# Making the high and low parts of the feed-forward weights with casting and accumulating DMAs

## The chip, the core and the metric

The kernel runs on one core of a Trainium2 chip. The core has TensorE (PE in the profile) for matrix multiplies, VectorE (DVE) and ScalarE (ACT) for elementwise work, GpSimd (POOL) for small odd work, and SyncE (SP), which here only issues DMAs. Each engine works through its own queue in order, and they meet through semaphores. Sixteen DMA engines move data between memory and the on-chip SBUF. POOL can issue DMAs too. The metric is the time of one execution on the device, in microseconds.

## The reference

One transformer-like block over 512 tokens of width 1024, in float32:

```python
h = rms_norm(x, norm1_g[l])
proj = h @ w_in[l]
...
merged = (jax.nn.sigmoid(g_ssd) * (y_ssd @ w_ssd_proj[l])
          + jax.nn.sigmoid(g_attn) * (y_attn @ w_attn_proj[l]))
x = x + merged @ w_out[l]
h2 = rms_norm(x, norm2_g[l])
u = causal_dwconv(h2 @ w_up[l], ffn_conv_w[l], ffn_conv_b[l])
u_gate, u_val = jnp.split(u, 2, axis=-1)
x = x + (jax.nn.silu(u_gate) * u_val) @ w_down[l]
```

The first half has a state-space branch and a windowed attention branch. The change touches only the weights of the last part, the feed-forward: w_up (1024 by 5632) and w_down (2816 by 1024).

## The kernel before

All large products are made with three matrix multiplies in the type float32r, a float32 with a shortened mantissa: each operand is split into a high part, its value rounded to float32r, and a low part, the rest. The product is high·high + high·low + low·high, summed in one PSUM bank. Activations are split once and stay in SBUF (h2h and h2l after the second norm, acth and actl after the gate). Weights are streamed.

The stream is a list of *pieces* of 512 KB (128 partitions by 1024 values), in the order in which TensorE uses them. Pieces 0 to 127 belong to the earlier stages, 128 to 171 to w_up (128 columns each, read from memory in rows of 128 values), 172 to 193 to w_down (256 rows by 512 columns each, in rows of 512 values). `load_piece` (L85) loads a piece through SP's queue into a tile called raw. `make_piece` (L91) casts it on ACT to the high part whi (L100) and subtracts on DVE to the low part wlo (L101). Each of the three kinds of tile has three buffers, so a piece's parts take the places of the piece three before it. `prefetch` (L104) is called in the middle of a piece's matmuls and makes pieces up to one ahead of the next; `next_piece` hands a piece to the matmuls.

In an **up stage** (`mm_chan`, L135) one piece is 24 matmuls of 512 columns into one PSUM bank: eight of high weight and high activation, eight of high and low, eight of low weight and high activation. The high part is thus free after two thirds of the piece, the low part at its end. The bank is emptied by `conv3` (L989): ACT writes facc from it (L991), DVE adds two shifted products from the bank (L995, listed at L52). Then ACT applies silu (L1012), or DVE multiplies the two halves (L1015), ACT casts (L1016) and DVE subtracts (L1017) to give acth and actl. Four PSUM banks (the tag "mm") go round among the blocks. In a **down stage** (`mm_tok`, L886) a piece is used for four blocks of tokens in four banks, six matmuls each; the last two pieces of each half are used together, block by block.

Ahead of the first up stage stands the second norm. For each of four blocks of tokens: DVE adds to x, ACT squares and sums (L923), DVE makes a mean (L930, L201), POOL takes the power −1/2 (rs, in `rstd`, L202), DVE scales (hn), TensorE transposes (tr_h), ACT and DVE make h2h and h2l (L211, L212). TensorE's order is written out by hand throughout; DVE's and ACT's order is by hand in the second norm. Everything else, POOL's and SP's queues among it, is put in order by a scheduler at build time.

Of the kernel before, what the change touches and what calls it, by code (L numbers as in the profile page):

```python
# [8 lines left out]
F32 = mybir.dt.float32  # L9
F32R = mybir.dt.float32r  # L10
AF = mybir.ActivationFunctionType
ALU = mybir.AluOpType
# [26 lines left out]
def kernel(  # L39
# [6 lines left out]
    nc = tc.nc  # L46
# [7 lines left out]
    def pool(name, side="left", bufs=1):  # L54
        return tc.tile_pool(name=name, bufs=bufs, side=side, reuse_waits="tile")

    cp = ctx.enter_context(pool("const"))
    wp = ctx.enter_context(pool("weights"))
# [7 lines left out]
    def chan_piece(w, c0, n, k0=0, nk=KD):  # L66
        return w[k0 * P:(k0 + nk) * P, c0:c0 + n].rearrange("(k p) c -> p k c", p=P)

    pieces = []
# [7 lines left out]
    pieces += [chan_piece(w_attn_proj, m * 256, 256, 0, 4) for m in range(4)]  # L77
    pieces += [chan_piece(w_ssd_proj, m * 512, 512, k, 2) for m in range(2) for k in range(0, 16, 2)]
    pieces += [chan_piece(w_out, n * 512, 512, k, 2) for n in range(2) for k in range(0, KD, 2)]
    pieces += [chan_piece(w_up, i * DFF + m * P, P) for m in range(NF) for i in range(2)]  # L80
    pieces += [chan_piece(w_down, n * 512, 512, k, 2) for n in range(2) for k in range(0, NF, 2)]
    raws, made = [], []
    used = [0]

    def load_piece():  # L85
        n = len(raws)
        raw = wp.tile([P, pieces[n].shape[1], pieces[n].shape[2]], F32, tag="raw", name=f"raw{n}", bufs=3)
        nc.sync.dma_start(raw, pieces[n])
        raws.append(raw)

    def make_piece():  # L91
        n = len(made)
        if n == len(pieces):
            return
        if n == len(raws):
            load_piece()
        raw, shape = raws[n], list(raws[n].shape)
        hi = wp.tile(shape, F32R, tag="whi", name=f"whi{n}", bufs=3)
        lo = wp.tile(shape, F32R, tag="wlo", name=f"wlo{n}", bufs=3)
        nc.scalar.copy(hi, raw)  # L100
        nc.vector.tensor_sub(lo, raw, hi.bitcast(F32))  # L101
        made.append((hi, lo))

    def prefetch(n=2):  # L104
        while len(made) < min(used[0] + n, len(pieces)):
            make_piece()

    def next_piece(ahead=1):
        i = used[0]
        used[0] += 1  # L110
        while len(made) < min(i + 1 + ahead, len(pieces)):
            make_piece()
        return made[i]
# [21 lines left out]
    def mm_chan(ps, w, xh, xl, c=0, n=P, nk=KD, t0=0, nt=S, ticks=True, lo_first=False):  # L135
        hi, lo = w
        i, total = 0, 3 * nk
        for a, b in ((hi, xh), (lo, xh), (hi, xl)) if lo_first else ((hi, xh), (hi, xl), (lo, xh)):
            for k in range(nk):
                nc.tensor.matmul(ps[:, t0:t0 + nt], a[:, k, c:c + n], b[:, k, t0:t0 + nt],  # L140
                                 start=(i == 0), stop=(i == total - 1))
                i += 1
                if ticks and i == 12 and total > 12:
                    prefetch()
                    tick()
# [248 lines left out]
    def proj_tok(g, name, fin, first=False):  # L394
# [9 lines left out]
        if first:  # L404
            used[0] = 2
            with tc.manual_schedule(engines={mybir.EngineType.DVE, mybir.EngineType.Activation}):
                first_norm(0)
                warm(3, "b")
                first_scale(0, 0)
                make_piece()  # L410
                first_norm(1)
                first_t(0, 0)
# [41 lines left out]
        for kq in range(3 if first else 0, 4):  # L454
            w = next_piece()
            for b in range(NT):
                part(b, kq, w)
                if kq == 3:
                    fin(b, pss[b])
                if b == 1:  # L460
                    prefetch()
                if b % 2:
                    tick()
# [374 lines left out]
    with pool("ysplit") as sp:  # L838
# [14 lines left out]
        for m4 in range(2):  # L853
            pss = [bank("mm", f"ps_sp{m4}_{j}") for j in range(4)]
            for k2 in range(8):
                hi, lo = next_piece()
                ys = split_y(8 * m4 + k2)
                split_y(8 * m4 + k2 + 1)
                for j in range(4):
                    if j == 2:  # L860
                        prefetch()
                    cs = slice(j * P, (j + 1) * P)
                    for i, (w, xi) in enumerate(((hi, 0), (hi, 1), (lo, 0))):
                        for k in range(2):
                            nc.tensor.matmul(pss[j], w[:, k, cs], ys[k][xi],  # L865
                                             start=(k2 == 0 and i == 0 and k == 0),
                                             stop=(k2 == 7 and i == 2 and k == 1))
            for j in range(4):
                m = m4 * 4 + j
                nc.vector.tensor_mul(gt[:, m, :], gt[:, m, :], pss[j])  # L870
                nc.vector.tensor_add(gt[:, m, :], gt[:, m, :], gt[:, 8 + m, :])
                nc.scalar.copy(mh[:, m, :], gt[:, m, :])
                nc.vector.tensor_sub(ml[:, m, :], gt[:, m, :], mh[:, m, :].bitcast(F32))
# [184 lines left out]
```

## Time and profile before

| | |
|---|---|
| median of the timed runs | 1242.08 us (1242.03 to 1242.13, two runs) |
| the profiled execution | 1242.08 us, span 1240.3 us |
| granted TensorE clock, mean | 0.997 |
| up stage in the profile | 872.2 to 1116.6 us |
| down stage in the profile | 1116.6 to 1236.6 us |
| pieces loaded there | 44 of w_up, 22 of w_down, 512 KB each |

The span is the time between the first and the last instruction; the 1.8 us between it and the time of the execution lie around it. "Busy" for TensorE counts matmuls that overlap one another. In a table of windows, each engine has its busy time and the number of its instructions; then follow the granted TensorE clock, the share of time that the 16 DMA engines were busy, and GB/s. In the order of time, a row has its start, its length, the engine, the line, the operation with its tiles, and in square brackets how long the engine sat idle before and what ended that.

### The profile page before, as it was taken

To read this page: it belongs to the slowest core of one execution; us is meant where nothing else is said; L and a number is where in the kernel's file an instruction comes from. 1 tells how busy PE (TensorE), PEld (TensorE's weight loads), DVE (VectorE), ACT (ScalarE), POOL (GpSimd) and SP (SyncE) were. 2 spreads that over 40 slices of the span, in tenths; PEclk is the share of its full clock that TensorE was granted. 3 is DMA by queue.
4 is the path that set the end of the run, shared out by engine and by line. 5 is a ranking of instruction groups with operands and counts; after the bars stand their busy time and mean duration, and the time that the engine had idled before them with its cause. 6 is when DMAs were issued, how large, how long until landed. Compare 5 with 4: busy or idle time off the path is not lost.

```text
span 1240.3 us, 15062 instructions
## 1 busy us (share of the span) xinstructions
PE 1227.8 (99%) x5944; PEld 1025.0 (83%) x5944; DVE 713.6 (58%) x955; ACT 557.8 (45%) x847; POOL 95.1 (8%) x77
## 2 busy tenths in 40 slices
PE   9998999999999999999999999999999999999998
PEld 7887888898788888888888888888888888888887
DVE  5345555655688988677843544654756656563222
ACT  4343554646675646566333324423544444442210
POOL 2030112220000111010102000000000000000000
PEclk9998999999999999999999999999999999999999
DMA  5422222222536644344233522252233333332330
GB/s 181 119 68 74 67 66 55 68 54 67 158 101 186 173 121 135 84 120 135 70 86 99 156 102 87 101 186 86 85 103 94 94 102 89 99 102 87 109 127 34
DMA packets 152535, 128.12 MB, mean 103 GB/s; under 512 B 10368, under 2 KB 123632, under 8 KB 151441
## 3 DMA queue, kind: packets, MB, share of 16 engines
q1 hardware_dynamic: 152465, 127.16, 34.7%
q8 instruction: 47, 0.77, 0.3%
q14 instruction: 23, 0.19, 0.0%
HBM read 124.73 MB, written 2.41 MB: 103 GB/s over the span
## 4 chain that ended last, share of the span: by engine, by line
PE 96%; DVE 2%; POOL 1%; ACT 1%; issue 0%; POOLq 0%; ACTq 0%
PE ps_ssd L140 21%; PE ps_u L140 20%; PE ps_wd L892 10%; PE ps_qk L400 10%; PE ps_gate L140 7%; PE ps_sp L865 7%; PE ps_v L400 5%; PE ps_wo L892 4%; PE ps_s L503 2%; PE ps_ap L140 2%; PE ps_pv L530 1%; PE ps_y L713 1%; PE ps_pt L519 1%; PE ps_o L718 1%; POOL qrs L202 1%; PE ps_st L694 1%
## 5 line engine op out<-in xcount | busy, mean ns | idle before, releaser
L101 DVE TENSOR_TENSOR wlo<-raw,whi 128x1024 fp32r<-128x1024 f32 x194 | 242.9, 1254 | 338.8 <-ACT whi L100 212.8
L100 ACT CAST whi<-raw 128x1024 fp32r<-128x1024 f32 x194 | 203.3, 1049 | 318.7 <-PE ps_wd L892 79.8
L140 PE MATMUL ps_ssd<-hl,whi 128*128 128x512 f32 x384 | 103.4, 398 | 0.0
L140 PE MATMUL ps_ssd<-hh,whi 128*128 128x512 f32 x384 | 98.6, 399 | 0.0
L140 PE MATMUL ps_ssd<-hh,wlo 128*128 128x512 f32 x384 | 95.3, 390 | 0.0
L140 PE MATMUL ps_u<-h2h,whi 128*128 128x512 f32 (+1 forms) x368 | 88.7, 383 | 0.3 <-ACT h2h L211 0.2
L140 PE MATMUL ps_u<-h2h,wlo 128*128 128x512 f32 (+1 forms) x368 | 88.1, 382 | 0.0
L140 PE MATMUL ps_u<-h2l,whi 128*128 128x512 f32 (+1 forms) x368 | 88.1, 381 | 0.0
L140 PEld LDWEIGHTS ps_ssd<-hh,wlo 128*128 128x128 f32 x384 | 72.1, 188 | 15.8
L140 PEld LDWEIGHTS ps_ssd<-hh,whi 128*128 128x128 f32 x384 | 71.0, 188 | 14.3 <-issue 0.2
L140 PEld LDWEIGHTS ps_ssd<-hl,whi 128*128 128x128 f32 x384 | 70.3, 188 | 13.9 <-issue 0.6
L140 PEld LDWEIGHTS ps_u<-h2h,whi 128*128 128x128 f32 x368 | 67.1, 188 | 14.5 <-ACT h2h L211 0.8
L140 PEld LDWEIGHTS ps_u<-h2l,whi 128*128 128x128 f32 x368 | 67.1, 188 | 14.0
L140 PEld LDWEIGHTS ps_u<-h2h,wlo 128*128 128x128 f32 x368 | 67.2, 188 | 13.7
L400 PE MATMUL ps_qk<-whi,hh 128*128 128x512 f32 x192 | 69.4, 443 | 0.0
L52 DVE SCALAR_TENSOR_TENSOR facc<-ps_u,sc,facc 128x511 f32<-128x511 f32 x88 | 65.8, 747 | 5.8 <-ACT facc L991 4.3
L400 PE MATMUL ps_qk<-whi,hl 128*128 128x512 f32 x192 | 60.3, 395 | 0.0
L400 PE MATMUL ps_qk<-wlo,hh 128*128 128x512 f32 x192 | 60.2, 395 | 0.0
L202 POOL TENSOR_TENSOR qrs<-qss,nhalf 128x8 f32<-128x8 f32 x24 | 45.8, 1908 | 178.6 <-DVE qss L201 178.6
L514 ACT ACTIVATE s<-s,st 128x128 f32<-128x128 f32 (+1 forms) x96 | 40.1, 419 | 36.0 <-DVE st L510 35.9
L892 PE MATMUL ps_wd<-whi,acth 128*128 128x512 f32 x176 | 54.2, 389 | 0.0
L892 PE MATMUL ps_wd<-wlo,acth 128*128 128x512 f32 x176 | 54.2, 389 | 0.0
(240 smaller groups left out, 2104.6 us busy)
## 6 DMA issues: line engine op xcount, KB each, us to landing
raw<-in_w_in_dram SPq DMA_DIRECT2D x100, 512.0 KB
raw<-in_w_up_dram SPq DMA_DIRECT2D x44, 512.0 KB
raw<-in_w_down_dram SPq DMA_DIRECT2D x22, 512.0 KB
bc<-scr_a SPq DMA_DIRECT2D x8, 1024.0 KB
raw<-in_w_ssd_proj_dram SPq DMA_DIRECT2D x16, 512.0 KB
eb<-scr_e SPq DMA_DIRECT2D x16, 256.0 KB
raw<-in_w_out_dram SPq DMA_DIRECT2D x8, 512.0 KB
fb<-scr_f SPq DMA_DIRECT2D x24, 128.0 KB
```

What stands on the lines that cost most here:

```text
L52: nc.vector.scalar_tensor_tensor(o, a, s, b, op0=op0, op1=op1)
L100: nc.scalar.copy(hi, raw)
L101: nc.vector.tensor_sub(lo, raw, hi.bitcast(F32))
L140: nc.tensor.matmul(ps[:, t0:t0 + nt], a[:, k, c:c + n], b[:, k, t0:t0 + nt], start=(i == 0), stop=(i == total - 1))
L202: return nc.gpsimd.tensor_tensor(rs, ss, nhalf.broadcast_to(tuple(ss.shape)) if ss.shape[1] > 1 else nhalf, op=ALU.pow)
L400: nc.tensor.matmul(pss[b], tok(g, kq * 2 + k, b, xx), w[:, k, :], start=(kq == 0 and j == 0 and k == 0), stop=(kq == 3 and j == 2 and k == 1))
L503: nc.tensor.matmul(ps[:, i * 2 * n:(i + 1) * 2 * n], qt[:, j, (b + i) * P:(b + i + 1) * P], kz[:, j, :, k0 + i * P:k0 + i * P + n], start= ...
L514: nc.scalar.activation(s3[:, 2 * i + h], s3[:, 2 * i + h], AF.Exp, bias=st[:, b + i, 0, 2 * j + h:2 * j + h + 1], accum_out=st[:, b + i, 1 ...
L519: nc.tensor.transpose(pst[:, o:o + P], s[:, o:o + P], ident)
L530: nc.tensor.matmul(pso[h * 64:(h + 1) * 64, (b + i) * P:(b + i + 1) * P], vt[:, b + i - nk + 1 + kb, (2 * j + h) * 64:(2 * j + h + 1) * 64 ...
L865: nc.tensor.matmul(pss[j], w[:, k, cs], ys[k][xi], start=(k2 == 0 and i == 0 and k == 0), stop=(k2 == 7 and i == 2 and k == 1))
L892: nc.tensor.matmul(pss[b], xx[:, k0 + k, b * P:(b + 1) * P], ww[:, k, :], start=(k0 == 0 and j == 0 and k == 0), stop=(k0 == nk - 2 and j ...
```

## The change

From piece 128 on, a piece is no longer loaded into raw and split by ACT and DVE. POOL issues a DMA from memory that casts to float32r while it writes the high part; ACT writes the low part's tile as −1 times the high part; POOL issues a second DMA of the same source that adds to that tile, which leaves source minus high part. The two parts take turns through all nine buffers of whi, wlo and raw, so that the high part of piece n takes the place of the low part of piece n−5, and its low part that of the high part of piece n−4. Between the fifth piece of w_up and the fourth from the end, `prefetch` makes one piece more.

```diff
+    first_up = len(pieces)
     pieces += [chan_piece(w_up, i * DFF + m * P, P) for m in range(NF) for i in range(2)]
...
     def make_piece():
         n = len(made)
         if n == len(pieces):
+            return
+        if n >= first_up:
+            src = pieces[n]
+
+            def part(i):
+                tag = ("whi", "wlo", "raw")[(2 * (n - first_up) + i) % 3]
+                t = wp.tile(list(src.shape), F32 if tag == "raw" else F32R, tag=tag, name=f"{tag}{n}", bufs=3)
+                return t.bitcast(F32R) if tag == "raw" else t
+            hi, lo = part(0), part(1)
+            nc.gpsimd.dma_start(hi, src)
+            nc.scalar.mul(lo, hi.bitcast(F32), -1.0)
+            nc.gpsimd.dma_start(lo, src, accum_op=ALU.add)
+            made.append((hi, lo))
             return
...
     def prefetch(n=2):
+        if first_up + 4 <= used[0] < len(pieces) - 4:
+            n += 1
         while len(made) < min(used[0] + n, len(pieces)):
             make_piece()
```

Line numbers of the changed program are higher by 14 or 16 behind this place: L104 is the casting DMA, L105 the multiply, L106 the accumulating DMA, L218 is rs (L202 before), L1007 facc (L991), L1028 silu, L1032 the cast to acth. In names the number of the piece stands behind whi, wlo or raw, and the last number is the builder's; a high or a low part can be in a tile of any of the three names.

The end of POOL's queue before, from the gates to the second norm (rs2_0 to rs2_3 are the four blocks' powers); nothing follows it:

```order
L813 COPY gt_5304<-bct_gate_5025 128x1024
L813 COPY gt_5304<-xst_gate_5026 128x1024
L813 COPY gt_5304<-zs_gate_5027 128x1024
L202 TENSOR_TENSOR rs2_0_6696<-ss2_0_6695,nhalf_77 128x1
L202 TENSOR_TENSOR rs2_1_6719<-ss2_1_6718,nhalf_77 128x1
L202 TENSOR_TENSOR rs2_2_6754<-ss2_2_6753,nhalf_77 128x1
L202 TENSOR_TENSOR rs2_3_6793<-ss2_3_6792,nhalf_77 128x1
```

The same place on POOL now:

```order
L104 DMA raw129_6799<-in_w_up_dram 128x8x128
L104 DMA whi128_6674<-in_w_up_dram 128x8x128
L106 DMA wlo128_6675<-in_w_up_dram 128x8x128
L218 TENSOR_TENSOR rs2_0_6695<-ss2_0_6694,nhalf_77 128x1
L218 TENSOR_TENSOR rs2_1_6718<-ss2_1_6717,nhalf_77 128x1
L104 DMA wlo130_6868<-in_w_up_dram 128x8x128
L218 TENSOR_TENSOR rs2_2_6753<-ss2_2_6752,nhalf_77 128x1
L104 DMA whi131_6960<-in_w_up_dram 128x8x128
L106 DMA whi129_6800<-in_w_up_dram 128x8x128
L218 TENSOR_TENSOR rs2_3_6792<-ss2_3_6791,nhalf_77 128x1
```

The first low part stands ahead of the first power, two high parts and a low part stand between the second and the fourth.

In the middle of the up stages POOL was empty; now it repeats these six rows (L104 a high part, L106 a low part):

```order
L104 DMA whi155_7774<-in_w_up_dram 128x8x128
L104 DMA raw156_7808<-in_w_up_dram 128x8x128
L106 DMA wlo155_7775<-in_w_up_dram 128x8x128
L106 DMA whi156_7809<-in_w_up_dram 128x8x128
L104 DMA wlo157_7846<-in_w_up_dram 128x8x128
L106 DMA raw157_7847<-in_w_up_dram 128x8x128
```

The low part of 156 stands directly ahead of the high part of 157, and the low part of 157 directly behind it.

ACT's queue at that place before, where the cast of piece 155 stands behind the work on block 11_1:

```order
L100 CAST whi154_7797<-raw154_7795 128x1024
L991 ACTIVATE facc11_1_7774<-ps_u11_1_7708,sc_85 128x512
L1016 CAST acth_6947<-facc11_1_7774 128x512
L100 CAST whi155_7832<-raw155_7830 128x1024
L991 ACTIVATE facc12_0_7813<-ps_u12_0_7781,sc_85 128x512
L1012 ACTIVATE facc12_0_7813<-facc12_0_7813 128x512
L100 CAST whi156_7871<-raw156_7869 128x1024
```

And now, where the multiplies stand in the casts' stead:

```order
L105 ACTIVATE wlo155_7775<-whi155_7774 128x1024
L1007 ACTIVATE facc11_1_7753<-ps_u11_1_7689,sc_85 128x512
L105 ACTIVATE whi156_7809<-raw156_7808 128x1024
L1032 CAST acth_6944<-facc11_1_7753 128x512
L1007 ACTIVATE facc12_0_7791<-ps_u12_0_7760,sc_85 128x512
L1028 ACTIVATE facc12_0_7791<-facc12_0_7791 128x512
L105 ACTIVATE raw157_7847<-wlo157_7846 128x1024
```

The multiply of piece 155 has moved ahead of the emptying of block 11_1's bank, and that of piece 156 ahead of block 12_0's; the order of the other rows is as it was.

## The prediction

> **What bounds the kernel now.** I read the page's busy times first, then busy time and granted clock of the two feed-forward stages, the chain that ended last, and the order of time inside one up stage.
>
> ```profile
> PE 1227.8 (99%) x5944; PEld 1025.0 (83%) x5944; DVE 713.6 (58%) x955; ACT 557.8 (45%) x847; POOL 95.1 (8%) x77
> ...
> core 0: us, PE busy (x) PEld busy (x) DVE busy (x) ACT busy (x) POOL busy (x), PEclk, DMA share, GB/s
> 872.20:1116.60 244.40, 244.13 (x1120) 202.46 (x1121) 150.91 (x185) 110.68 (x140) 1.47 (x1) 1.00 0.33 97
> 1116.60:1236.60 120.00, 120.00 (x530) 99.05 (x528) 31.94 (x31) 21.45 (x21) 0.00 (x0) 1.00 0.27 90
> ...
> 880.28 236.66 PE ps_u L140 x1056
> 1116.94 119.71 PE ps_wd L892 x528
> ```
>
> The last two rows are the end of the chain: TensorE alone. It is idle 1240.3 − 1227.8 = 12.5 us in the whole span, and 0.27 us in the 364 us that the change touches, at a granted clock of 1.00. So what DVE and ACT are spared there buys at most 0.3 us: it lies under matmuls. The question is only whether the new supply of weights keeps up with TensorE. One piece of w_up and its neighbours on ACT:
>
> ```profile
> 962.96 2.00 PE L140 MATMUL ps_u<-h2h,whi 128*128 128x512 f32 x8
> 963.16 0.78 ACT L991 ACTIVATE facc<-ps_u,sc 128x512 f32<-128x512 f32 x1 [0.79 <-PE ps_u L140]
> ...
> 966.64 0.62 ACT L1016 CAST acth<-facc 128x512 fp32r<-128x512 f32 x1 [2.70 <-DVE facc L1015]
> 967.17 1.04 ACT L100 CAST whi<-raw 128x1024 fp32r<-128x1024 f32 x1
> ...
> 968.45 2.00 PE L140 MATMUL ps_u<-h2h,whi 128*128 128x512 f32 x8
> ```
>
> The same group of eight matmuls returns after 968.45 − 962.96 = 5.49 us. In each such slot the program before loads 512 KB once, through SP, and ACT and DVE make the parts; SP is far ahead and nothing waits for a load.
>
> **What is removed and what is added.** Gone for 66 pieces are ACT's cast, DVE's subtraction and SP's load. ACT gets a multiply by −1 of the same shape, which I price as the cast, 1.05 us. POOL gets two transfers a piece, and the second waits for the multiply, which waits for the first to land:
>
> ```profile
> L100 ACT CAST whi<-raw 128x1024 fp32r<-128x1024 f32 x46 | 48.1, 1047 | 4.5 <-PE ps_u L140 4.5
> L101 DVE TENSOR_TENSOR wlo<-raw,whi 128x1024 fp32r<-128x1024 f32 x45 | 55.2, 1227 | 70.3 <-PE ps_u L140 67.9 <-ACT whi L100 2.3
> ```
>
> DVE loses 66 × 1.227 = 81 us, ACT nothing; both gains are worth 0 by the first paragraph. The cost is on POOL, whose queue is in order. Its rows in the up stage (the section on the change) repeat every three pieces: high n, high n+1, low n, low n+1, high n+2, low n+2. A low part's transfer holds the queue until its own high part has landed and been negated, so three pieces contain two trips that nothing else on POOL can overlap: low n+1 waits for high n+1, and low n+2 for high n+2. With L from a transfer's issue to its landing, g for the time POOL spends on issuing one, and two hand-offs of 0.1 us (DVE to POOL in the rows of the start below: 0.17 us), the loop is
>
> 2 (L + 1.05 + 0.20) + 3 g, against 3 × 5.49 = 16.47 us.
>
> Below that, TensorE sees nothing; above it, every three pieces lose the difference. The break is at 2L + 3g = 13.97 us.
>
> *g.* No transfer goes out through POOL in this trace. Nearest rows:
>
> ```profile
> L88 SPq DMA_DIRECT2D raw<-in_w_up_dram x44: 367/368/368, 844.7 to 1085.3; - x44
> L813 POOL COPY gt<-zs_gate 128x1024 f32<-128x1024 f32 x1 | 1.0, 1039 | 0.0
> L202 POOL TENSOR_TENSOR qrs<-qss,nhalf 128x8 f32<-128x8 f32 x24 | 45.8, 1908 | 178.6 <-DVE qss L201 178.6
> ```
>
> SP spends 0.37 us on the same piece; POOL needs 1.04 us to pass over a tile of that size and 1.91 us for its dearest repeated instruction. I take 1.5 us, between the two POOL rows, since the engine is POOL; bounds 0.37 and 1.91 (a larger g is a rival).
>
> *L.* The only loads that somebody visibly waits for are the first ones:
>
> ```profile
> 1.20 0.36 SPq L217 DMA_DIRECT2D ysb<-in_x_dram  x1
> ...
> 2.07 0.47 SPq L217 DMA_DIRECT2D ysb<-in_x_dram  x1
> ...
> 4.82 1.06 ACT L242 ACTIVATE ysb<-ysb 128x1024 f32<-128x1024 f32 x1 [2.75 <-DMA ysb<-in_x_dram]
> ...
> 7.53 1.06 ACT L242 ACTIVATE ysb<-ysb 128x1024 f32<-128x1024 f32 x1 [0.31 <-DMA ysb<-in_x_dram]
> ```
>
> 512 KB landed 4.82 − 1.20 = 3.62 us after issue with an empty queue, 7.53 − 2.07 = 5.46 us with three loads ahead. With POOL's g in place of SP's 0.36 the empty-queue value is 3.62 − 0.36 + 1.5 = 4.76 us. To this comes the wait behind other transfers. A plain piece takes 0.33 × 5.49 = 1.81 us of the 16 DMA engines (the share 0.33 above). The accumulating one reads its destination besides its source: between 1.81 us, if that is free, and 3.62 us, if each read counts; I take the middle, 2.7 us, since the second read is on the chip. Then high n+1 stands behind a low and a high part sent 2g earlier (2.7 + 1.81 − 3.0 = 1.5 us) and high n+2 behind a low part sent g earlier (2.7 − 1.5 = 1.2 us): 1.35 us on the mean, so L = 6.1 us.
>
> The loop is then 2 × 7.35 + 4.5 = 19.2 us, 2.73 us too long, and the 44 pieces of w_up hold about 14 loops: 38 us. ACT's multiply now waits for a landing at a place ahead of the facc that empties a PSUM bank, so ACT lags and TensorE, which wants the bank, is stalled through ACT. The banks put part of the payment off: four of them let ACT lag, and when the down stage opens all four within one piece, the lag is paid there. That changes the place, not the sum. The down stage itself I count at 0: its rows alternate high n+2, low n+1, so a trip has two pieces, 10.9 us, for L + 1.25 + 2g = 10.35 us.
>
> The Trainium skill ("Collectives: The Full Stack", on why ReduceScatter is half of AllGather) says that an add in the DMA engines costs no cycles of its own but doubles the reads, and that the rate halves. By that the accumulating transfer takes the upper bound of 3.62 us, the mean wait is 2.3 us, L 7.0, the loop 21.1 us, and 65 + 5 us are added instead of 38 + 5. No run here shows it.
>
> **The start.** Second norm's small POOL instructions now stand among these transfers.
>
> ```profile
> 858.66 1.05 ACT L100 CAST whi<-raw 128x1024 fp32r<-128x1024 f32 x1 [4.38 <-PE ps_wo L892]
> 862.61 0.63 ACT L923 ACTIVATE junk<-x 128x512 f32<-128x512 f32 x1 [2.90 <-DVE x L921]
> 863.57 0.15 DVE L201 TENSOR_SCALAR ss<-ss 128x1 f32<-128x1 f32 x1
> 863.89 0.55 POOL L202 TENSOR_TENSOR rs<-ss,nhalf 128x1 f32<-128x1 f32 x1 [190.33 <-DVE ss L201]
> 865.74 0.74 DVE L52 SCALAR_TENSOR_TENSOR hn<-x,rs,gb 128x512 f32<-128x512 f32 x1
> 867.08 1.03 PE L208 MATMUL tr_h<-ident,hn 128*128 128x128 f32 x8
> 872.79 0.63 ACT L923 ACTIVATE junk<-x 128x512 f32<-128x512 f32 x1
> 877.94 1.01 PEld L140 LDWEIGHTS ps_u<-h2h,wlo 128*128 128x128 f32 x8
> ```
>
> High part 128 can go when TensorE frees its buffer, at 858.66 as the cast did, and lands at 863.4; its multiply is ahead of the square at 862.61 in ACT's queue and ends at 864.5. Low part 128 then holds POOL until 866.1, where the first rs stood at 863.89: 2.2 us late, with 0.6 us of slack between the scale's end (866.48) and the transposes: 1.6 us of stall. Low part 129 is negated behind the square at 872.79, which now ends at about 875.2 with its sum, so the multiply ends at 876.2 and it lands 4.76 + 0.9 us later, at 881.9; TensorE wants it at 877.94 + 1.6 = 879.5: 2.4 us. With the third and fourth rs behind high parts 130 and 131, under 1 us more, I count 5 us.
>
> The sum against the profiled execution's own 1242.08 us (span 1240.3; the median of the two runs is the same): 1242.08 + 38 + 5 = 1285 us. With g 1.91 and the accumulate at 3.62, L is 6.8, the loop 21.9 and the total 1323; with g 1.2 and the accumulate at 2.2, L is 5.8, the loop 17.6 and the total 1263. That is the forecast's own range.
>
> **Rivals.**
> *The loop fits.* At the low ends, L = 3.62 and g = 0.37, it is 10.9 us; even g = 1.04 with an empty queue, L = 4.3, gives 14.2 us. Then only the start is paid: 1242 + 2 to 5, 1244 to 1247 us, not slower. It decides as soon as 2L + 3g stays under 13.97 us. For it: the DMA engines are busy 0.33 now, and 0.33 + 0.49 is not full. Against: it needs nearly no queueing beside an accumulate. The Trainium skill ("DMA: Bandwidth & Descriptors", Anatomy of one DMA) is on this side: it puts a transfer sent from GpSimd at 2.0 us plus bytes over 436 GB/s, an estimate of 3.2 us here, and calls descriptor generation small; by that rule the time is this rival's. The first load's 3.62 us agrees roughly, and nothing here shows a transfer from POOL.
> *POOL's issue or the DMA engines become the bound.* A piece of w_up moves in rows of 128 values, 1024 of them. If POOL spends 4 us on writing them out, its queue alone needs 8 us of every 5.49: 2.5 × 44 = 110 us, 1357. If the cast doubles a transfer as the accumulate does, the engines need 2 × 3.62 = 7.24 us a piece: 1.75 × 44 = 77 us and some 10 in the down stage, 1334. It decides from g = 2.75 us, or 5.49 us of transfer a piece. For it: POOL is the slow engine of this trace (1.9 us for 128x8). Against: no row shows a price of that size. I give it 1320 to 1400.
> *Faster.* The 0.3 us cannot show; one small row helps (rs at 874.89 took 1.47 us beside DVE's subtraction, the others 0.55, and the subtraction is gone):
>
> ```profile
> 874.89 1.47 POOL L202 TENSOR_TENSOR rs<-ss,nhalf 128x1 f32<-128x1 f32 x1 [4.03 <-DVE ss L201]
> ```
>
> Should the casting transfer not round, the values change and no duration does.
>
> **How the numbers follow.** Forecast 0.44, fitting loop 0.27, POOL or DMA bound 0.28, faster 0.01. A measurement here tells about 2% from no change, so 1267 us divides: the fitting loop and 0.03 of the forecast lie below. Faster 0.01, same 0.30, slower 0.69. The range leaves out the lower part of the fitting loop (0.07) and the dearest of the last case (0.13): 1244 to 1390.
>
> **What would show it.** Right: in the up stage POOL waits for ACT before each low part, two long waits in three pieces; ACT waits for transfers ahead of facc; TensorE's idle time is released by facc or by a low part, some 2.7 us in three pieces, and at the first matmuls of the down stage; the DMA share there rises from 0.33 to about 0.75. The fitting loop: TensorE idle only before 885 us. POOL's bound: transfers leave POOL back to back without waits, or the DMA share stands near 1. Wrong outright: TensorE stalls on anything before 858 us, or DVE does not lose its 81 us.

## The result, and the profile after

The changed kernel takes 1348.97 us (median of two runs, 1348.46 to 1349.48) against 1242.08 us: 1.086 times as long, with a 95% interval of 1.0834 to 1.0886. The profiled execution has a span of 1346.7 us against 1240.3 us, 106.4 us more.

From the page of the changed kernel: the busy times and the row of POOL's DMA queue (packets, MB, and the time that they took as a share of 16 engines' span).

```profile
PE 1263.0 (94%) x5944; PEld 1038.7 (77%) x5944; DVE 636.9 (47%) x889; ACT 554.2 (41%) x847; POOL 245.1 (18%) x209
...
q0 software_dynamic: 103488, 69.21, 33.0%
```

DVE lost 713.6 − 636.9 = 76.7 us of work, as intended. TensorE makes the same 5944 matmuls and is now idle 1346.7 − 1263.0 = 83.7 us instead of 12.5 us. Three places can be read from the order of time on TensorE: the first matmul of piece 130 (the first with 512 columns), the first of the down stage, and the last, whose end closes the down stage. Before:

```profile
886.05 2.00 PE L140 MATMUL ps_u<-h2h,whi 128*128 128x512 f32 x8
...
1116.77 0.62 PE L892 MATMUL ps_wd<-whi,acth 128*128 128x512 f32 x2
...
1236.01 0.61 PE L892 MATMUL ps_wd<-wlo,acth 128*128 128x512 f32 x2
```

After, with the long waits at the opening of the down stage:

```profile
884.52 1.81 PE L156 MATMUL ps_u<-h2h,whi 128*128 128x256 f32 x8 [2.85 <-DMA whi<-in_w_up_dram]
...
894.01 2.00 PE L156 MATMUL ps_u<-h2h,wlo 128*128 128x512 f32 x8
...
1203.41 0.70 PE L908 MATMUL ps_wd<-wlo,acth 128*128 128x512 f32 x2
...
1207.04 0.73 PE L908 MATMUL ps_wd<-raw,acth 128*128 128x512 f32 x2 [2.47 <-DMA raw<-in_w_down_dram]
1213.31 1.19 PE L908 MATMUL ps_wd<-wlo,acth 128*128 128x512 f32 x2 [5.54 <-DVE facc L52]
...
1224.59 0.77 PE L908 MATMUL ps_wd<-wlo,acth 128*128 128x512 f32 x1 [4.76 <-DVE facc L52]
...
1342.22 0.61 PE L908 MATMUL ps_wd<-raw,acth 128*128 128x512 f32 x2
```

| stretch | before | after | more | forecast |
|---|---|---|---|---|
| start, to piece 130 | 886.05 | 894.01 | 8.0 | 5 |
| up stage, 42 pieces | 230.7 | 309.4 | 78.7 | 38 |
| down stage | 119.8 | 139.4 | 19.6 | 0 |

In the up stage a piece takes 309.4 / 42 = 7.37 us instead of 5.49. The window of the up stage of the changed kernel (columns: length, busy time and count of PE, PEld, DVE, ACT, POOL, then granted clock, DMA share, GB/s):

```profile
884.00:1130.00 246.00, 208.40 (x845) 163.54 (x845) 68.56 (x94) 74.95 (x97) 76.95 (x63) 0.93 1.01 139
```

The DMA share is 1.01 in the up stage (0.32 before), and the granted clock is 0.93 there (1.00 before). The waits of the changed kernel (engine, tile and line, what was waited for: total, times, longest):

```profile
DVE facc L52 <- ACT facc L1007: 219.0, 37, 9.3
...
POOL raw L106 <- ACT raw L105: 121.1, 22, 9.7
...
POOL wlo L106 <- ACT wlo L105: 105.5, 20, 7.5
ACT wlo L105 <- DMA whi<-in_w_up_dram: 70.6, 12, 9.4
...
PE ps_u L156 <- DVE facc L52: 29.7, 9, 3.5
```

POOL waits for ACT's multiply, the multiply for the landing of the high part, DVE for ACT, which stands at that multiply, and TensorE for a bank that DVE has not read yet. One loop of three pieces on POOL, in order of time, from one low part to the low part three pieces later:

```profile
1015.06 1.53 POOL L106 DMA_DIRECT2D raw<-in_w_up_dram  x1 [8.46 <-ACT raw L105]
1015.95 1.57 POOL L104 DMA_DIRECT2D whi<-in_w_up_dram  x1
1016.83 1.57 POOL L104 DMA_DIRECT2D raw<-in_w_up_dram  x1
1024.73 1.56 POOL L106 DMA_DIRECT2D wlo<-in_w_up_dram  x1 [6.33 <-ACT wlo L105]
1026.43 1.54 POOL L106 DMA_DIRECT2D whi<-in_w_up_dram  x1
1027.33 1.55 POOL L104 DMA_DIRECT2D wlo<-in_w_up_dram  x1
1037.32 1.53 POOL L106 DMA_DIRECT2D raw<-in_w_up_dram  x1 [8.44 <-ACT raw L105]
```

And ACT's multiplies in the same stretch:

```profile
1023.29 1.06 ACT L105 ACTIVATE wlo<-whi 128x1024 fp32r<-128x1024 f32 x1 [5.65 <-DMA whi<-in_w_up_dram]
1024.25 0.76 ACT L1007 ACTIVATE facc<-ps_u,sc 128x512 f32<-128x512 f32 x1
1025.08 1.06 ACT L105 ACTIVATE whi<-raw 128x1024 fp32r<-128x1024 f32 x1
```

The loop takes 1037.32 − 1015.06 = 22.26 us. It has two trips, as the prediction said. The first goes from the issue of high n at 1015.95 to its multiply, which starts on landing at 1023.29, and to the issue of low n at 1024.73: 8.78 us. The second, from high n+2 at 1027.33 to low n+2 at 1037.32, takes 9.99 us. What lies between is 3.49 us: two issues that follow the one before after 0.89 and 0.90 us (an issue is 1.55 us long here, but the next begins while it lasts), and 1.70 us from low n to low n+1, whose multiply stands behind a facc.

This is one of the shorter loops. Only every second piece ends in a silu, and in every second loop that silu stands between the two multiplies too and waits for DVE. ACT and POOL in such a loop:

```profile
951.76 1.06 ACT L105 ACTIVATE wlo<-whi 128x1024 fp32r<-128x1024 f32 x1 [5.22 <-DMA whi<-in_w_up_dram]
952.73 0.76 ACT L1007 ACTIVATE facc<-ps_u,sc 128x512 f32<-128x512 f32 x1
955.15 0.63 ACT L1028 ACTIVATE facc<-facc 128x512 f32<-128x512 f32 x1 [1.66 <-DVE facc L52]
955.68 1.05 ACT L105 ACTIVATE whi<-raw 128x1024 fp32r<-128x1024 f32 x1
...
953.12 1.56 POOL L106 DMA_DIRECT2D wlo<-in_w_up_dram  x1 [6.40 <-ACT wlo L105]
957.12 1.54 POOL L106 DMA_DIRECT2D whi<-in_w_up_dram  x1 [2.44 <-ACT whi L105]
```

From low n to low n+1 it is then 957.12 − 953.12 = 4.00 us, and that loop, 943.37 to 967.89 us, takes 24.52 us. The eleven loops between 943.37 and 1201.37 us take 258.0 / 11 = 23.45 us on the mean. Ahead of them TensorE loses nothing: between 894 and 941 us it is busy 47.00 of 47.00 us.

This leaves two theories. **Q**: POOL's in-order queue with its two trips in three pieces sets the pace. **E**: the DMA engines are full. E has a strong number on its side. In the start, where each transfer stands alone, the DMA view of two stretches of 7 us of the changed kernel gives the share of the 16 engines and, at the end of the second row, the time from issue to landing in us; the casting one first (858 to 865 us):

```profile
q0 software_dynamic: 1040, 0.52, 40.8%
...
whi<-in_w_up_dram POOLq DMA_DIRECT2D x1, 512.0 KB, 4.7
```

and the accumulating one (865 to 872 us):

```profile
q0 software_dynamic: 1040, 0.52, 61.6%
...
wlo<-in_w_up_dram POOLq DMA_DIRECT2D x1, 512.0 KB, 6.5
```

That is 0.408 × 7 = 2.86 us and 0.616 × 7 = 4.31 us of all engines, 7.17 us a piece, and a piece took 7.37 us on the mean of the stage, with a DMA share of 1.01. The experiments had to tell this from the loop.

### The profile page after: what moved, and what is told of

Its sections match the earlier page's. It is cut to its first block, busy times and chain, and to the rows that moved or that the text cites. A ratio compares the mean times of both kernels' runs of the same rounds, so it can differ in the third digit from the quotient of the medians.

```text
span 1346.7 us, 15061 instructions
## 1 busy us (share of the span) xinstructions
PE 1263.0 (94%) x5944; PEld 1038.7 (77%) x5944; DVE 636.9 (47%) x889; ACT 554.2 (41%) x847; POOL 245.1 (18%) x209
## 4 chain that ended last, share of the span: by engine, by line
PE 70%; issue 18%; POOL 7%; DVE 2%; DMA 1%; ACT 1%; POOLq 0%; ACTq 0%; DVEq 0%
PE ps_ssd L156 20%; PE ps_qk L416 9%; PE ps_wd L908 9%; PE ps_gate L156 6%; PE ps_sp L881 6%; PE ps_v L416 5%; PE ps_wo L908 2%; PE ps_s L519 2%; PE ps_ap L156 2%; POOL wlo L106 2%; POOL raw L104 2%; POOL wlo L104 1%; PE ps_pv L546 1%; PE ps_y L729 1%; PE ps_pt L535 1%
## 5 line engine op out<-in xcount | busy, mean ns | idle before, releaser
L115 DVE TENSOR_TENSOR wlo<-raw,whi 128x1024 fp32r<-128x1024 f32 x128 | 163.2, 1277 | 192.6 <-ACT whi L114 137.7
L114 ACT CAST whi<-raw 128x1024 fp32r<-128x1024 f32 x128 | 134.0, 1048 | 230.4 <-PE ps_ssd L156 62.6
L156 PE MATMUL ps_u<-h2h,whi 128*128 128x512 f32 (+1 forms) x256 | 72.2, 431 | 38.0 <-DVE facc L52 29.7
L156 PEld LDWEIGHTS ps_u<-h2h,whi 128*128 128x128 f32 x256 | 51.8, 214 | 53.5 <-issue 22.2
L218 POOL TENSOR_TENSOR qrs<-qss,nhalf 128x8 f32<-128x8 f32 x24 | 45.8, 1907 | 179.7 <-DVE qss L217 179.7
L156 PE MATMUL ps_u<-h2h,wlo 128*128 128x512 f32 (+1 forms) x240 | 61.0, 397 | 11.9 <-issue 8.3
L105 ACT ACTIVATE wlo<-whi 128x1024 fp32r<-128x1024 f32 x22 | 23.3, 1058 | 117.2 <-DMA whi<-in_w_up_dram 70.6
L156 PE MATMUL ps_u<-h2h,raw 128*128 128x512 f32 (+1 forms) x240 | 59.3, 389 | 5.6 <-DMA raw<-in_w_up_dram 5.6
L156 PEld LDWEIGHTS ps_u<-h2h,wlo 128*128 128x128 f32 x240 | 43.6, 191 | 26.4 <-issue 12.5
L105 ACT ACTIVATE raw<-wlo 128x1024 fp32r<-128x1024 f32 x22 | 23.3, 1060 | 94.4 <-DMA wlo<-in_w_up_dram 54.6
L156 PEld LDWEIGHTS ps_u<-h2h,raw 128*128 128x128 f32 x240 | 43.3, 188 | 18.4 <-DMA raw<-in_w_up_dram 9.9
```

Of the source, the lines that this page charges most:

```text
L105: nc.scalar.mul(lo, hi.bitcast(F32), -1.0)
L218: return nc.gpsimd.tensor_tensor(rs, ss, nhalf.broadcast_to(tuple(ss.shape)) if ss.shape[1] > 1 else nhalf, op=ALU.pow)
```

## The experiments

In each group of runs the kernel before ran on the same chip: 1242.2 to 1242.3 us throughout. Ratios are to it, with 95% intervals.

### late_low: an edit that did not do what it was meant to

The low parts are emitted apart from the high parts, and POOL's transfers are chained in the order of the code:

```diff
+    lows, sent = [], []
+
+    def make_low():
+        n = first_up + len(lows)
+        hi, lo = made[n]
+        nc.scalar.mul(lo, hi.bitcast(F32), -1.0)
+        with tc.issue_after(sent[-1].ins):
+            sent.append(nc.gpsimd.dma_start(lo, pieces[n], accum_op=ALU.add))
+        lows.append(n)
...
-            nc.gpsimd.dma_start(hi, src)
-            nc.scalar.mul(lo, hi.bitcast(F32), -1.0)
-            nc.gpsimd.dma_start(lo, src, accum_op=ALU.add)
+            with tc.issue_after(sent[-1].ins) if sent else nullcontext():
+                sent.append(nc.gpsimd.dma_start(hi, src))
             made.append((hi, lo))
+            if n - first_up >= 2:
+                make_low()
...
             make_piece()
+        while first_up + len(lows) <= i:
+            make_low()
```

> Both transfers of every piece stay, but POOL sends the low part of piece n only after the high part of piece n+2, so no low part waits directly behind its own high part. Theory E, the DMA engines are the bound (alone in their queue a casting transfer took 0.408 x 7 us = 2.86 us of all 16 engines and an accumulating one 0.616 x 7 = 4.31 us, 7.2 us a piece of w_up against TensorE's 5.49): the up stage stays at about 7.2 us a piece, DMA share near 1, 1325 to 1350 us. Theory Q, POOL's queue is the bound (two trips of high part, multiply, low part in three pieces, 2 x (7.4 + 1.25) + 3 x 1.55 = 21.95 us, 7.3 a piece): the trips are gone, 5.5 us a piece, 1245 to 1255 us.

Measured: 1519.21 us, 1.2227 (1.2207 to 1.2248). The added loop in `next_piece` let the low parts catch up at once, so from piece 130 on each low part stood directly behind its own high part: not the late order of the expectation but a fully serial one, with one trip per piece. POOL in order of time (here L115 casts and L99 adds):

```profile
919.89 1.53 POOL L99 DMA_DIRECT2D whi<-in_w_up_dram  x1 [7.12 <-ACT whi L97]
920.78 1.57 POOL L115 DMA_DIRECT2D wlo<-in_w_up_dram  x1
929.18 1.54 POOL L99 DMA_DIRECT2D raw<-in_w_up_dram  x1 [6.83 <-ACT raw L97]
```

A piece takes 9.29 us here and 9.72 us the next time: an issue, then a trip of 8.40 us, and of 8.84 us the next time. The run doesn't decide what its expectation was about. It does show that a longer chain of trips with the same transfers is slower by far, which the same engines' capacity alone would not make it.

### add_only and cast_only: half of the change each

add_only keeps SP's load and ACT's cast and makes only the low part by the multiply and the accumulating DMA; cast_only makes the high part by the casting DMA, loads raw by SP and lets DVE subtract. In both the three kinds of tile have three buffers each again, as in the kernel before (lines not shown).

```diff
 # add_only
-            nc.gpsimd.dma_start(hi, src)
+            nc.scalar.copy(hi, raw)
             nc.scalar.mul(lo, hi.bitcast(F32), -1.0)
             nc.gpsimd.dma_start(lo, src, accum_op=ALU.add)
 # cast_only
             nc.gpsimd.dma_start(hi, src)
-            nc.scalar.mul(lo, hi.bitcast(F32), -1.0)
-            nc.gpsimd.dma_start(lo, src, accum_op=ALU.add)
+            nc.vector.tensor_sub(lo, raw, hi.bitcast(F32))
```

> The accumulating transfer alone: SP loads raw and ACT casts as in the kernel before, ACT writes -1 times the high part, POOL sends only the accumulating transfer. POOL has no trip left. Theory E: 1.81 (plain load) + 4.31 = 6.12 us a piece, 0.63 over, 44 pieces, 28 us and some for the start and for three buffers a kind instead of nine in turn: 1268 to 1295 us. Theory Q: nothing on POOL waits for POOL, 1242 to 1250 us.

> The casting transfer alone: POOL casts the high part, SP loads the same source plain into raw, DVE subtracts. Theory E: 2.86 + 1.81 = 4.67 us a piece fits in 5.49, 1242 to 1250 us, DMA share about 0.85 in the up stage. Theory Q: no trip, the same time. Above 1262 us both fall, and a transfer from POOL would be dear for another reason.

Measured: add_only 1255.79 us, 1.0108 (1.0093 to 1.0124), between the two theories; cast_only 1245.67 us, 1.0029 (1.0018 to 1.0041), as both expected. The windows of add_only from the second norm to the end of the down stage:

```profile
872.00:884.00 12.00, 7.96 (x59) 7.33 (x58) 6.01 (x12) 6.98 (x10) 3.67 (x3) 0.92 0.70 136
884.00:896.00 12.00, 12.00 (x73) 11.32 (x72) 2.88 (x4) 6.42 (x8) 1.54 (x1) 0.79 0.46 83
896.00:1116.00 220.00, 220.00 (x962) 180.50 (x962) 88.54 (x122) 133.78 (x163) 63.29 (x41) 1.00 1.12 196
1116.00:1236.00 120.00, 115.25 (x500) 94.53 (x499) 9.10 (x13) 47.02 (x47) 23.88 (x20) 0.99 0.80 180
```

TensorE loses 4.0 us in the start, then a stretch at a clock of 0.79, and 4.75 us in the down stage. Between them it is busy 220.00 of 220.00 us, with the DMA share at 1.12. So a share about 1 doesn't say that the engines hold up the work: here a higher one than the changed kernel's goes with no loss at all.

### long_rows: fewer, longer rows

The pieces of w_up are read as rows of 512 values instead of 128, from other places of the matrix, so other values are computed (the tiles are viewed in the same shape for both transfers, lines not shown).

```diff
+            if n < first_up + 2 * NF:
+                m = n - first_up
+                src = chan_piece(w_up, m // 4 * 512, 512, m % 4 * 2, 2)
```

> As the changed kernel, but each piece of w_up is read as 256 runs of 512 values, as w_down is, in place of 1024 runs of 128 (the same number of bytes from the same matrix, other values than the computation asks for). Theory E: if the engines' time goes with the number of rows, it falls from 7.2 us a piece to what the down stage shows (0.912 x 100 us over 35 transfers, 5.2 us a piece), under 5.49: 1250 to 1275 us; if it goes with the bytes, 1340 to 1350 us. Theory Q: landing falls to the down stage's 5.8 us and issue to 1.0: 2 x 7.05 + 3 = 17.1 us a loop, 0.6 over, 1255 to 1265 us.

Measured: 1327.56 us, 1.0684 (1.0653 to 1.0716). No expectation held: the gain was small. Its window of the up stage:

```profile
884.00:1130.00 246.00, 213.71 (x888) 170.40 (x888) 75.03 (x103) 80.42 (x105) 66.13 (x68) 0.94 0.70 146
```

The DMA share is 0.70 and the stage is still slow, which speaks against E. Against the size that Q gave: I had let L shrink with the rows, and it hardly did. The casting transfers land after a median of 7.7 us (8.1 in the changed kernel), and the trips on POOL are nearly as long:

```profile
1006.15 1.23 POOL L110 DMA_DIRECT2D whi<-in_w_up_dram  x1
...
1015.51 1.21 POOL L112 DMA_DIRECT2D wlo<-in_w_up_dram  x1 [7.39 <-ACT wlo L111]
```

This trip takes 9.36 us and the next 8.77 us; eleven loops take 22.2 us on the mean (23.45 in the changed kernel).

### late2: the late order, this time as meant

The edit of late_low with one other condition:

```diff
-            if n - first_up >= 2:
+            if first_up + len(lows) <= n - 2:
                 make_low()
```

POOL's order in the up stage is now high n+2, low n, high n+3, low n+1. `make_low` emits ACT's multiply together with the low part, so the multiply too comes later, and not POOL's order alone has changed.

> The same 132 transfers, the same sizes and row lengths; only POOL's order differs: in the steady part of the up stage it is now high n+2, low n, high n+3, low n+1, so a low part stands two pieces behind its own high part (some 11 us) and no trip is waited for on POOL. If POOL's in-order trips set the pace (theory Q), the loop is gone, POOL needs only two issues of 1.55 us a piece, and what stays is the start (7.6 us in the changed kernel): 1245 to 1262 us. If the DMA engines' capacity sets it (theory E: 2.86 + 4.31 = 7.2 us of engines a piece against 5.49), the order changes nothing in the up stage: 1325 to 1350 us. If the engines are only partly short (their busy shares overlap), between: 1262 to 1300 us.

Measured: 1261.82 us, 1.0162 (1.0147 to 1.0177). With the same transfers in another order, 87 of the 107 us are gone. ACT, which waited for landings ahead of facc in the changed kernel, does so only twice between 900 and 1110 us, 4.5 us in all. No run moves the multiply on ACT's queue without the low part on POOL's, or the other way round, so their shares stay open. The windows of late2:

```profile
872.00:884.00 12.00, 4.25 (x24) 3.15 (x23) 5.75 (x11) 2.84 (x5) 2.62 (x3) 0.76 0.35 44
884.00:896.00 12.00, 6.31 (x36) 6.10 (x35) 1.38 (x2) 2.13 (x3) 3.38 (x3) 0.78 0.39 50
896.00:1130.00 234.00, 233.44 (x1040) 193.22 (x1041) 92.68 (x127) 101.49 (x130) 104.66 (x87) 0.99 1.30 194
```

From 896 us on TensorE is busy, at a DMA share of 1.30. What is left is the start, where it is idle 13.4 us in 24 and at a clock of 0.76 to 0.78, and it is longer than the changed kernel's: the first low part now stands behind three powers of the norm and goes out at 876.3 us, where it went at 865.7.

### late2_rows and no_add: the two prices inside the loop

late2_rows joins the late order and the long rows. no_add keeps the changed kernel's order and lets the second transfer cast without adding, so the low parts are not residuals.

```diff
 # no_add
-            nc.gpsimd.dma_start(lo, src, accum_op=ALU.add)
+            nc.gpsimd.dma_start(lo, src)
```

> The order of the run before, and the pieces of w_up read as rows of 512 values instead of 128 (so the weights are taken from other places and other values are computed). Alone in the queue such a cast took 2.05 us of the engines and such an add 3.37 us in the earlier run with long rows, 5.4 us a piece, and each issue 1.2 us. Theory Q: 1245 to 1255 us, since neither trips nor engines are short. Theory E: 5.4 us just fits into 5.49, so 1245 to 1265 us too; the two part in the pair of this run with the long rows in the old order (1327.6 us): by E order cannot matter there.

> POOL's order and waits stay as in the changed kernel, but the second transfer only casts and does not add (the low parts are then not residuals: the subtraction is left out). Measured alone, a cast takes 2.86 us of the engines and an add 4.31 us. Theory E: 2 x 2.86 = 5.7 us a piece against 5.49: 1250 to 1270 us. Theory Q: the two trips stay, each shorter by the 1.45 us that an add in front of it cost, so L falls from 7.4 to about 6.0 and the loop is 2 x 7.25 + 3 x 1.55 = 19.2 us for three pieces, 2.7 us too long, about 14 times, and the start: 1280 to 1300 us.

Measured: late2_rows 1261.49 us, 1.0158 (1.0141 to 1.0175). That is above Q's 1245 to 1255 us, which left out the start that late2 also pays, and inside E's 1245 to 1265. The pair decides: with long rows the order alone is worth 1327.56 − 1261.49 = 66 us, where E said that it cannot matter. In the late order the rows' length is worth nothing (1261.82 against 1261.49). no_add: 1291.46 us, 1.0396 (1.0380 to 1.0411), in the range of Q and beyond that of E. One loop of no_add on POOL:

```profile
991.95 0.88 POOL L104 DMA_DIRECT2D whi<-in_w_up_dram  x1
...
999.11 0.88 POOL L106 DMA_DIRECT2D wlo<-in_w_up_dram  x1 [5.40 <-ACT wlo L105]
...
1001.59 0.88 POOL L104 DMA_DIRECT2D wlo<-in_w_up_dram  x1
1009.53 0.88 POOL L106 DMA_DIRECT2D raw<-in_w_up_dram  x1 [7.06 <-ACT raw L105]
```

The trips are 7.16 and 7.94 us, where the loop shown of the changed kernel had 8.78 and 9.99. Eleven loops take 19.8 us on the mean instead of 23.45: 3.7 us less, of the 7.0 us that were too much. In time, 57.5 of the 107 us are gone with the add; the rest stays, as the trips do.

### down_only: w_down alone

```diff
-    first_up = len(pieces)
     pieces += [chan_piece(w_up, i * DFF + m * P, P) for m in range(NF) for i in range(2)]
+    first_up = len(pieces)
```

> The change for the 22 pieces of w_down alone; w_up goes by ACT and DVE as before. If the 19.7 us that the down stage lost in the changed kernel were a lag brought over from the up stage, nothing stays: 1242 to 1247 us. If the down stage itself is too slow (trips or engines), 1252 to 1265 us.

Measured: 1246.02 us, 1.0030 (1.0019 to 1.0041). With the change in the down stage alone 4 us are lost, not 19.6: most of what that stage lost in the changed kernel came with it from the up stage.

### late1, late2_start, late1_start, after_start: the distance and the start

late1 has n − 1 in the condition of late2: low n, high n+2, low n+1, high n+3. The three others make pieces 128 to 131 as before and start with the change at 132.

```diff
+    first_up += 4
     pieces += [chan_piece(w_down, n * 512, 512, k, 2) for n in range(2) for k in range(0, NF, 2)]
```

> POOL's steady order is low n, high n+2, low n+1, high n+3: a low part stands one piece nearer to its own high part than in the late order. From high n+2 to low n+2 there are then two periods, so the loop is 2 T = 0.9 (spacing of two issues) + L + 1.25. With L from 7.4 to 8.1 us T is 4.8 to 5.1 us a piece, under 5.49: by theory Q the up stage runs at TensorE's pace and only the start of the late order is paid, 1255 to 1270 us. If a trip of a whole piece's length still binds, or the engines do: over 1290 us.

> The late order, and the first four pieces of w_up (128 to 131) made by ACT and DVE as before, so that no transfer stands among second norm's small instructions on POOL. In the late order TensorE was idle about 13 us between 872 and 896 us and hardly anywhere else. If that start is all that the late order still loses: 1242 to 1249 us. If there is a price in the steady stage (engines, POOL): 1255 to 1262 us.

> The order with the shorter distance, and the first four pieces made as before. By theory Q 1242 to 1249 us, since 4.8 to 5.1 us a piece is under 5.49. If the shorter distance binds: over 1265 us.

> The changed kernel's order, and the first four pieces of w_up made as before. The start's 7.6 us go, and 4 of the 42 pieces that each lost 1.88 us (7.5 us): 1349 - 15 = 1334 us, between 1325 and 1342. If the start's delay were what sets the later pace: under 1300 us.

| kernel | us | ratio | 95% |
|---|---|---|---|
| late1 | 1260.92 | 1.0157 | 1.0141 to 1.0173 |
| late2_start | 1245.02 | 1.0025 | 1.0015 to 1.0035 |
| late1_start | 1243.16 | 1.0007 | 0.9998 to 1.0016 |
| after_start | 1341.09 | 1.0797 | 1.0779 to 1.0815 |

All four came out where Q had them. With the loop undone and the start made as before, the change costs nothing that can be measured (late1_start). With the start alone put right, it costs nearly all it did (after_start), though 7 us more than the 1334 us of its expectation. The up stage of late1_start, and a piece on POOL (L116 casts, L100 adds):

```profile
884.00:1130.00 246.00, 246.00 (x1089) 202.42 (x1088) 97.53 (x133) 107.17 (x136) 110.07 (x93) 1.00 1.26 194
```

```profile
1008.15 0.90 POOL L116 DMA_DIRECT2D whi<-in_w_up_dram  x1 [1.10 <-PE ps_u L170]
1009.71 1.55 POOL L100 DMA_DIRECT2D raw<-in_w_up_dram  x1 [0.65 <-ACT raw L98]
1013.59 0.89 POOL L116 DMA_DIRECT2D raw<-in_w_up_dram  x1 [2.33 <-PE ps_u L170]
```

Now POOL waits for TensorE to free a buffer, and briefly for ACT. A piece takes 5.44 us (1013.59 − 1008.15), with two transfers of the same kinds and sizes that took 7.17 us of engines when each stood alone; where the changed kernel moved 139 GB/s, this moves 194 GB/s. That settles E.

## Why the prediction was right or wrong

**Right: the direction and the place; the range by luck.** TensorE had nothing to gain; the loss came from POOL's queue, with two long waits for ACT in three pieces, ACT waiting for landings ahead of facc, and TensorE released by facc and at the opening of the down stage, as the last part of the prediction listed. DVE lost its work for nothing. That the order on POOL's and ACT's queues makes the loss, with the transfers as they were, is shown by late2, late1_start and after_start, not only argued. The time lies inside the whole range, 1244 to 1390 us, only because the case of the full DMA engines, which did not come, stretched it upwards; the forecast's own range ended at 1323.

**Wrong: the size, 1285 against 1349. Two terms of the loop failed: L was too small, and the way on ACT from one multiply to the next was put at nothing.** The loop was set at 7.35 + 7.35 us of trips and 4.5 us of issues, 19.2 us. The eleven loops of 23.45 us consist, on the mean, of 8.93 us from high n to low n, 2.89 from low n to low n+1, 9.85 from high n+2 to low n+2, and two issues of 0.89. L, up to the multiply's start, is 7.50 us for high n and 8.39 for high n+2 instead of 6.1: 3.7 us more in a loop. Low n+1 was to wait for the landing of high n+1. It waits for its multiply, which stands on ACT behind that of piece n, a facc and in every second loop silu: 2.89 us where a mere issue takes 0.89, 2.0 us more. The multiply with its hand-off, 1.44 us instead of 1.25, gives 0.4 more, and three issues of 0.89 instead of 1.5 give 1.8 less: 3.7 + 2.0 + 0.4 − 1.8 = 4.3 us, which is 23.45 − 19.2 but for rounding. Eleven loops that are 23.45 − 16.47 = 7.0 us too long give 77 of the up stage's 79 us; 14 of 2.73 gave the forecast's 38. That nothing is lost ahead of these loops fits after_start: it also spares four pieces, for which its expectation took off 7.5 us besides the start, and gained 7.9 us in all.

L was 4.76 us with an empty queue and 1.35 us behind others, 6.1 us. Its empty-queue part was right for a cast (4.7 us to landing, above). Its second part was not: it took the add at 2.7 us of engines, the middle between one and two plain loads, and the cast in front at 1.81 us, as a plain load. Alone they took 4.31 and 2.86 us. The median landing of the casting transfers in the up stage, 8.1 us, is near an estimate from the transfers standing alone: an add issued 0.89 us earlier lands 6.5 us after its issue, and the cast behind it needs its 2.86 us then, 6.5 − 0.89 + 2.86 = 8.5 us. That the add is part of it is shown by no_add, whose loops are 3.7 us shorter. For no_add the same way gives 4.7 − 0.87 + 2.86 = 6.7 us, against a median of 6.3. For long_rows, whose first transfers stand alone as well (an add lands after 5.9 us, a cast takes 0.293 × 7 = 2.05 us of the engines, issues follow after 0.74 us), it gives 7.2 us, against 7.7: longer rows spare less of L than that run's expectation took off, and the estimates miss by 0.4 to 0.5 us.

**g** was 1.5 us; the issue's duration is 1.55, but the queue moves on after 0.89. A duration in the profile wasn't the interval that the loop needed. This error went the other way and hid 1.8 us of the other two.

**The start**, forecast 5, was 8.0 us. The mechanism held: TensorE waits 2.85 us for the low part of piece 129, where the prediction had 2.4, and 0.85 + 0.61 + 0.93 us for the late transposes and what follows them. These waits are 5.2 us, near the forecast. The rest is no wait: between 884 and 896 us the granted clock is 0.86 (1.00 before), and eight matmuls of 256 columns last 1.81 us at 884.52 us instead of 1.10.

**The down stage**, forecast 0, was 19.6 us. The prediction said that the lag of the banks is paid there but "changes the place, not the sum". That was wrong: the loops alone make up the up stage's 79 us, and TensorE had the lag of the last blocks to wait for on top. The rows at its opening hold 2.47 + 5.54 + 4.76 = 12.8 us of waits, and one more holds 0.72. Most of the other 6 us is no wait either: twelve pairs of matmuls between 1213 and 1230 us follow each other after 0.76 to 0.99 us instead of 0.46, at a granted clock of 0.63 from 1203 to 1225 us. down_only, which has no such lag from a loop, loses 4 us in all.

**The rivals.** The case of the full DMA engines gave 1334 us from 7.24 us a piece, and the engines' time alone was 7.17 us: nearly the right number from the wrong cause. The DMA share near 1, which the prediction had named as that case's sign, was there too (1.01), and is no sign of it. late2 and late1, which leave all transfers as they are, tell the two apart, and so does the pair of long_rows and late2_rows. An issue of 4 us, the other half of that case, did not come: issues follow each other after 0.89 us. The fitting loop would have needed 2L + 3g under 13.97 us, with issues of 0.89 us an L of some 5.6 us. It was right about the engines' room and wrong about the trips.

**The two rules.** The Trainium skill ("Collectives: The Full Stack", why ReduceScatter is half of AllGather) says of the add in a ReduceScatter that it doubles the reads and halves the rate. Here the add took 4.31 / 2.86 = 1.5 times the cast's time, between its factor and none; the sum by it, 65 + 5 us, was nearer than the forecast's. "DMA: Bandwidth & Descriptors" (Anatomy of one DMA) of the Trainium skill gives 2.0 us and bytes over 436 GB/s, an estimate of 3.2 us. The traces here don't agree: 4.7 us for a cast with an empty queue and 6.5 us for an add, and it has no term for the transfer in front.

## What to carry to other kernels

When a queue that runs in order holds an instruction that waits for the landing of an earlier one in the same queue, count the round trips per unit of work before anything else, and put the dependent instruction, with the work that feeds it, one or two units later: the same 132 transfers cost 107 us in one order and 19 or 20 us in two others, and 1 to 3 us in these once the first eight were left out of a busy start. The price of such a trip is not the transfer's own time alone: the transfer ahead of it counts too (without the add a loop was 3.7 us shorter), and so does what stands on the other engine's queue between two such hand-overs (2.0 us a loop here). A busy share of the DMA engines near 1 is no proof that they are full; look whether the consumer waits, and change the order to see.

## What the runs showed of the hardware that was not expected

The DMA share rose to 1.26 with no stall (late1_start, 194 GB/s), so it is no share of a capacity; what it counts more than once isn't seen here. An accumulating DMA of 512 KB, in rows of 128 values, took 4.31 us of the engines, as the DMA view counts them, and a casting one 2.86, each alone in the queue: 1.5 times. And the issue of an accumulating transfer in rows of 128 values lasts 1.55 us in POOL's rows and that of a casting one 0.9 us (late1_start above), or 1.55 us too when it goes out right behind an accumulating one, while the next issue begins after 0.89 us (the changed kernel's loop).
